# Hymba layer, fp32 in three products: the last output tile's mixed activation blocks made between the products of the first gate/up pair, and the token scale one product later

## The chip, the cores and the metric

The kernel runs on one core of a Trainium2 chip. The metric is the device time of one execution in microseconds; the median of three runs of the kernel before is 2037.42 us (2037.31 to 2037.79).

## The reference

One decoder layer for 512 tokens of width 2048, with 16 learned tokens put ahead of them. Cut to what matters here:

```python
n = _rmsnorm(h, g_mix[l])
p = n @ w_in[l]                       # q, k, v | gb, gc, u
o_attn = _stick_breaking_attention(q, k, v)
o_conv = gb * _causal_dwconv(gc * u, conv_w[l])
o = jnp.concatenate([_rmsnorm(o_attn, g_attn_out[l]),
                     _rmsnorm(o_conv, g_conv_out[l])], axis=-1)
h = h + o @ w_out[l]
n2 = _rmsnorm(h, g_ffn[l])
h = h + (jax.nn.silu(n2 @ w_gate[l]) * (n2 @ w_up[l])) @ w_down[l]
```

## The kernel before

**Precision.** Every operand of a large product is split into a high part and a rest (hi, lo), and a product is three matmuls: hi by hi, hi by lo, lo by hi (lines 795, 796 and 797, each once per tile of 128 rows, so 24 matmuls for one block of eight tiles).

**Pairs.** The projections are done in pairs of 2 x 2 blocks of weights (a gate tile and an up tile in the feed-forward part, and two tiles of the convolution's projections), each pair with seven block products instead of eight. `pair_product` (L799) uses three PSUM banks, x, y and z. The product x(acts[2]) goes on adding to the bank x after the product x(acts[0]) in it was copied out, and so on: after x(acts[0]), z(acts[1]) and x(acts[2]) ScalarE copies the bank into `sides` (`read_out`, L811), and after z(acts[3]) and x(acts[4]) VectorE reads it into `out2` (L825, L829), the two halves of u. The last product, x(acts[6]), adds to the bank x again. Normal pairs go x0, z1, x2, z3, x4, y5, x6. The first convolution pair (i = 0) and the first gate/up pair (i = CONV) are "swapped": the product y(acts[5]) comes first.

**Weights.** A product's weights are made by `prepare` (L225), up to two products ahead (S_AHEAD), in three places of `sw_split` that are used in turn: SP loads a block of 512 KB (`load_quad`, L167), ScalarE rounds it to the high part (L202), VectorE subtracts for the low part (L203). The products 1, 2, 4 and 6 use sums of blocks, made by VectorE: t1 and t3 in `add_quads` (L209), t2 in L252, and t2 with the last block in L219. Each block's load for the next pair is put on SP behind the last sum that reads the block (`load_next`, L183). The steps run at high priority, and a scheduler sets the order in which each engine's queue gets them, unless the code pins it. Seven weights steps of a swapped pair come in the order 5, 0, 1, 2, 3, 4, 6 (L223).

**The output projection's tiles.** They are walked in the order of OUT_TILES (L938). For each, the residual is added (L980 to L984), scaled by g_ffn into `src` (L986), and the blocks of the feed-forward part's seven activations acts[0] to acts[6] are made: plain ones, differences and sums of the four quarter blocks, each split into hi and lo (`split_f`, L990, over L324). Blocks 4 and 6 go through DRAM (`fx`) and are loaded by POOL (`load_f`, L919). For the last tile, i = KT - 1 = 15, with the banks po15x, po15y and po15z, all this runs in one piece at the highest priority (L1007 to L1012): residual, `mixed_blocks` (L997) with acts 0, 1, 2, then 3 and 4, and the sum of squares (L345) for the feed-forward part's norm.

**The token scale.** `h_scale` (L1044) splits that sum (L324, tile work_r), has PE sum it over the partitions (ss_h, L673 and L676), and makes the reciprocal root with VectorE and ScalarE. In the first gate/up pair it is called after the product z(acts[3]) (L826); the result scales g and u in `gate` (L1072).

## Time and profile before

| | us |
|---|---|
| median of three runs | 2037.42 |
| the profiled execution, its own time | 2037.97 |
| its span in the trace | 2036.1 |
| around the span | 1.9 |
| first gate/up pair, first matmul | 767.35 |
| third gate/up pair, first matmul | 811.29 |

PE is TensorE's matmul stream, PEld its weight loads, DVE VectorE, ACT ScalarE, POOL GpSimd, SP the queue that issues the weights' loads. A row of the timeline has the start and the length in us, the engine, the line of the kernel, the operation, out<-in, and the shape; what stands in brackets at its end is the idle time before it and what released it. A row of the waits has the total in us, how often, and the longest. All times of the trace count from the start of the span. The ends of matmuls are modelled (0.28 us of length at a pace of 0.11), so matmuls are timed from start to start.

### The profile page before, as it was taken

The page shows a single profiled execution, that of the slowest core. Times are in us where ns is not written, and L with a number is a line of the kernel's source. Part 1 is how long each engine was busy: PE and PEld are TensorE (multiplying, and loading weights), DVE is VectorE, ACT ScalarE, POOL GpSimd, SP SyncE. Part 2 cuts the span into 40 slices and gives each one's busy share as a digit, 9 for nine tenths or more (in the row PEclk, how much of TensorE's full clock was granted, in tenths as well). Part 3 has the DMA queues.
Part 4 walks back from the last instruction along what each step waited for, and adds up shares of the span by engine and source line. Part 5 has one row for each costly group of instructions (what it writes and reads, how often), then busy time and mean ns, then how long its engine had stood idle before and what let it go on. Part 6 is the DMA issues. An engine that isn't in the chain of part 4 may idle for free.

```text
span 2036.1 us, 39674 instructions
## 1 busy us (share of the span) xinstructions
PE 2022.7 (99%) x16158; PEld 1962.6 (96%) x16158; DVE 1728.1 (85%) x2196; ACT 1078.8 (53%) x1556; POOL 337.9 (17%) x507
## 2 busy tenths in 40 slices
PE   9999999999999999999999999999999999999999
PEld 8999999899998889999999999999999999999999
DVE  7877777698878778998988988988998978888887
ACT  7776766344454445555555555555555544444443
POOL 0111111200014440111111110110110242131211
PEclk9999999999999999999999999999999999999999
DMA  6343344833355556556555555555555999797864
GB/s 221 102 140 123 125 136 136 270 104 107 104 205 175 167 160 203 146 171 181 149 168 160 152 168 157 154 168 156 158 166 153 283 340 349 170 313 200 220 151 89
DMA packets 156087, 356.30 MB, mean 175 GB/s; under 512 B 13632, under 2 KB 67648, under 8 KB 155136
## 3 DMA queue, kind: packets, MB, share of 16 engines
q1 hardware_dynamic: 72208, 216.76, 33.4%
q0 software_dynamic: 83696, 136.99, 25.1%
q8 instruction: 127, 2.08, 0.4%
q14 instruction: 56, 0.46, 0.1%
HBM read 275.78 MB, written 77.92 MB: 174 GB/s over the span
## 4 chain that ended last, share of the span: by engine, by line
PE 92%; DVE 3%; DMA 2%; ACT 1%; issue 1%; POOL 0%; SPq 0%; DVEq 0%; ACTq 0%; POOLq 0%
PE x L795 13%; PE x L797 13%; PE x L796 13%; PE z L795 7%; PE z L796 7%; PE z L797 7%; PE y L796 3%; PE y L797 3%; PE y L795 3%; PE pv L311 2%; PE pv L312 2%; PE pv L313 2%; PE pk L312 1%; PE pk L311 1%; PE pk L313 1%; PE pq L313 1%
## 5 line engine op out<-in xcount | busy, mean ns | idle before, releaser
L202 ACT CAST sw_split<-sw_in 128x1024 fp32r<-128x1024 f32 (+2 forms) x668 | 661.7, 992 | 709.8 <-PE z L796 193.3
L203 DVE TENSOR_TENSOR sw_split<-sw_in,sw_split 128x1024 fp32r<-128x1024 f32 (+2 forms) x668 | 777.8, 1165 | 149.2 <-ACT sw_split L202 144.3
L797 PE MATMUL x<-f,sw_split 128*128 128x256 f32 x1408 | 387.4, 275 | 0.4 <-DVE sw_split L203 0.4
L795 PE MATMUL x<-f,sw_split 128*128 128x256 f32 x1408 | 387.4, 275 | 0.1
L796 PE MATMUL x<-f,sw_split 128*128 128x256 f32 x1408 | 387.3, 275 | 0.0
L797 PEld LDWEIGHTS x<-f,sw_split 128*128 128x128 f32 x1408 | 264.3, 188 | 0.6 <-DVE sw_split L203 0.6
L795 PEld LDWEIGHTS x<-f,sw_split 128*128 128x128 f32 x1408 | 264.3, 188 | 0.5 <-ACT sides L811 0.5
L796 PEld LDWEIGHTS x<-f,sw_split 128*128 128x128 f32 x1408 | 264.3, 188 | 0.0
L1066 POOL DMA_DIRECT2D fd<-s x147 | 103.7, 922 | 710.8 <-DVE s L324 710.0
L209 DVE TENSOR_TENSOR sw_in<-sw_in 128x1024 f32<-128x1024 f32 (+1 forms) x164 | 187.9, 1146 | 13.1 <-DMA sw_in<-w_in 5.0
L797 PE MATMUL z<-f,sw_split 128*128 128x256 f32 x704 | 193.8, 275 | 1.7 <-DVE sw_split L203 1.7
L795 PE MATMUL z<-f,sw_split 128*128 128x256 f32 x704 | 193.9, 275 | 1.5 <-ACT sides L811 1.3
L796 PE MATMUL z<-f,sw_split 128*128 128x256 f32 x704 | 193.7, 275 | 0.0
L797 PE MATMUL x<-ring,sw_split 128*128 128x256 f32 x608 | 167.3, 275 | 0.5 <-DVE sw_split L203 0.5
L795 PE MATMUL x<-ring,sw_split 128*128 128x256 f32 x608 | 167.2, 275 | 0.0
L796 PE MATMUL x<-ring,sw_split 128*128 128x256 f32 x608 | 167.2, 275 | 0.0
L797 PEld LDWEIGHTS z<-f,sw_split 128*128 128x128 f32 x704 | 132.2, 188 | 1.9 <-DVE sw_split L203 1.9
L795 PEld LDWEIGHTS z<-f,sw_split 128*128 128x128 f32 x704 | 132.2, 188 | 1.9 <-ACT sides L811 1.5
L796 PEld LDWEIGHTS z<-f,sw_split 128*128 128x128 f32 x704 | 132.2, 188 | 0.0
L797 PEld LDWEIGHTS x<-ring,sw_split 128*128 128x128 f32 x608 | 114.1, 188 | 0.7 <-DVE sw_split L203 0.7
L795 PEld LDWEIGHTS x<-ring,sw_split 128*128 128x128 f32 x608 | 114.1, 188 | 0.0
L796 PEld LDWEIGHTS x<-ring,sw_split 128*128 128x128 f32 x608 | 114.1, 188 | 0.0
(609 smaller groups left out, 5459.1 us busy)
## 6 DMA issues: line engine op xcount, KB each, us to landing
sw_in<-w_gu SPq DMA_DIRECT2D x176, 512.0 KB, 4.0
sw_in<-w_in SPq DMA_DIRECT2D x92, 512.0 KB, 3.4
fd<-s POOLq DMA_DIRECT2D x147, 256.0 KB, 5.3
sw_in<-w_down SPq DMA_DIRECT2D x96, 384.0 KB, 4.3
ring<-fd POOLq DMA_DIRECT2D x42, 768.0 KB, 16.8
sw_in<-w_out SPq DMA_DIRECT2D x32, 512.0 KB, 3.4
out_T<-d POOLq DMA_DIRECT2D x54, 256.0 KB, 4.7
mix_dram<-st_x POOLq DMA_DIRECT2D x16, 516.0 KB, 4.1
```

The source lines that it names most:

```text
L202: sc.copy(hi, src)
L203: ve.tensor_tensor(lo, src, hi.bitcast(F32), ALU.subtract)
L209: return ve.tensor_tensor(sums[name], a, b, ALU.add)
L311: pe.matmul(ps, wh, ah[:, a:b], start=k + i == 0, stop=False)
L312: pe.matmul(ps, wh, al[:, a:b], start=False, stop=False)
L313: pe.matmul(ps, wl, ah[:, a:b], start=False, stop=k + i == last)
L795: pe.matmul(p, hi[:, kk], ah, start=start and j == k == 0, stop=False, skip_group_check=skip)
L796: pe.matmul(p, hi[:, kk], al, start=False, stop=False, skip_group_check=skip)
L797: pe.matmul(p, lo[:, kk], ah, start=False, stop=k == n - 1, skip_group_check=skip)
L1066: gp.dma_start(fd[c][s][:, :, k], t[:, :, i])
```

## The change

The last tile's three mixed blocks are taken out of the one piece and put into a list, `between`: the third block (L1011 of the new file, for acts[2]), the fourth (L1015, acts[3]) and the fifth (L1021, acts[4], with the sum of squares behind it and the release of the buffers). `go_between` runs one after each of the pair's first three products, at high priority and queued behind `latest[0]`, which is the last low half of weights or the last t2 sum issued till then. The token scale runs after x(acts[4]) instead of after z(acts[3]). The pool that holds its work tiles opens when the fifth block is done, so g and u get a pool of their own. In the swapped pairs, both of them, the t3 sum and the last sum (with the loads behind them) are also queued behind `latest[0]`. The other output tiles run the same operations as before.

```diff
--- before.py
+++ after.py
@@ -151,6 +151,7 @@
     pieces += [("pair", i, s) for i in range(CONV, len(pairs)) for s in range(7)]
     quads, sums, split_w, used, wide, raws = {}, {}, [], [0], {}, []
     S_AHEAD = 2
+    latest = [None]
 
     def load_first(i):
 
@@ -200,7 +201,7 @@
             at = half * 8 * P
             hi, lo = (sw_split[:, at + i * 4 * P : at + (i * 4 + n) * P] for i in range(2))
         sc.copy(hi, src)
-        ve.tensor_tensor(lo, src, hi.bitcast(F32), ALU.subtract)
+        latest[0] = ve.tensor_tensor(lo, src, hi.bitcast(F32), ALU.subtract)
         split_w.append((hi, lo))
 
     def add_quads(i, name, a, b):
@@ -249,13 +250,14 @@
             elif s == 1:
                 split_quad(sums["t1"], n)
                 sums["t2"] = sums["t1"]
-                ve.tensor_tensor(sums["t2"], sums["t2"], b["22"], ALU.add)
+                latest[0] = ve.tensor_tensor(sums["t2"], sums["t2"], b["22"], ALU.add)
                 if not swapped:
                     add_t3(i, b)
             elif s == 2:
                 split_quad(sums["t2"], n)
                 if swapped:
-                    add_t3(i, b)
+                    with tc.issue_after(latest[0].ins):
+                        add_t3(i, b)
             elif s == 3:
                 split_quad(b["22"], n)
                 load_next(i, "22")
@@ -267,7 +269,8 @@
                     add_last(i, b)
             else:
                 if swapped:
-                    add_last(i, b)
+                    with tc.issue_after(latest[0].ins):
+                        add_last(i, b)
                 split_quad(sums["t2"], n)
                 if i + 1 == SIX:
                     load_quad(SIX + 1, QUADS[1])
@@ -796,7 +799,14 @@
                 pe.matmul(p, hi[:, kk], al, start=False, stop=False, skip_group_check=skip)
                 pe.matmul(p, lo[:, kk], ah, start=False, stop=k == n - 1, skip_group_check=skip)
 
-    def pair_product(acts, cols, out2, side, fourth=None):
+    between = []
+
+    def go_between():
+        if between:
+            with tc.high_priority(), tc.issue_after(latest[0].ins):
+                between.pop(0)()
+
+    def pair_product(acts, cols, out2, side, fifth=None):
 
 
 
@@ -815,18 +825,21 @@
         first = i in (0, CONV)
         if first:
             block_product(y, acts[5], True)
+            go_between()
         block_product(x, acts[0], True)
         read_out(p1, x)
+        go_between()
         block_product(z, acts[1], True)
+        go_between()
         read_out(p5, z)
         block_product(x, acts[2], False)
         read_out(u2, x)
         block_product(z, acts[3], False)
         ve.scalar_tensor_tensor(out2[0], z, -1.0, u2, ALU.mult, ALU.subtract)
-        if fourth:
-            fourth()
         block_product(x, acts[4], False)
         ve.scalar_tensor_tensor(out2[1], x, -1.0, p5, ALU.mult, ALU.subtract)
+        if fifth:
+            fifth()
         if not first:
             block_product(y, acts[5], True)
         return y, lambda: (block_product(x, acts[6], False), x)[1]
@@ -994,29 +1007,38 @@
             ve.tensor_tensor(src[:, 4], src[:, 3], src[:, 1], ALU.subtract)
             split_f(1, 4)
 
-        def mixed_blocks():
-            split_f(0, 0)
-            if i < KT - 1:
-                late_block()
+        def third_block():
             ve.scalar_tensor_tensor(src[:, 4], src[:, 4], -1.0, src[:, 0], ALU.mult, ALU.subtract)
             split_f(2, 4)
+
+        def fourth_block():
             ve.scalar_tensor_tensor(src[:, 5], src[:, 4], -1.0, src[:, 2], ALU.mult, ALU.subtract)
+            if i < KT - 1:
+                ve.tensor_tensor(src[:, 1], src[:, 0], src[:, 1], ALU.subtract)
+            split_f(3, 5)
+
+        def fifth_block():
             ve.tensor_tensor(src[:, 1], src[:, 0], src[:, 1], ALU.subtract)
+            split_f(4, 1)
+            square_sum(acc_h, hj, False, wide_tmp("h", bufs=2), ve)
+            hbuf.release()
+            nonlocal apool
+            apool = open_pool("apool")
 
         if i == KT - 1:
             with tc.high_priority(1 << 20):
                 residual(ve)
-                mixed_blocks()
-                split_f(3, 5)
-                split_f(4, 1)
-                square_sum(acc_h, hj, False, wide_tmp("h", bufs=2), ve)
+                split_f(0, 0)
+            between.extend([third_block, fourth_block, fifth_block])
         else:
             residual(gp if half else ve)
             if half:
                 split_f(5, 2)
             else:
-                mixed_blocks()
-                split_f(3, 5)
+                split_f(0, 0)
+                late_block()
+                third_block()
+                fourth_block()
             st = two(wide_tmp("st", F32R, 2))
             split(st[:, 0], st[:, 1], src[:, 3 if half else 1])
             gp.dma_start(fx[6 if half else 4][:, :, k], st)
@@ -1028,18 +1050,17 @@
         (gp if i < KT - 1 else nc.sync).dma_start(out[j], hj)
     assert not waiting
     acts = [acts[s] for s in range(7)]
-    hbuf.release()
-
-    def ffn_pair(acts, c1, c2, fourth=None):
+
+    def ffn_pair(acts, c1, c2, fifth=None):
 
         cols = c1.shape[-1]
         side = [sides[:, n * T2 : n * T2 + cols] if cols == T2 or not n else c2[:, 2 - n] for n in range(3)]
         views = [lambda part, k, t=t: t[:, part, k] for t in acts]
-        y, last = pair_product(views, cols, [c2[:, t] for t in range(2)], side, fourth)
+        y, last = pair_product(views, cols, [c2[:, t] for t in range(2)], side, fifth)
         ve.tensor_tensor(c1[:, 0], y, side[0], ALU.add)
         return last()
 
-    apool = open_pool("apool")
+    gu_pool = open_pool("gu_pool")
 
     def h_scale():
         w = apool.tile([P, 5, SEQ], F32R, tag="s5", name="work_r")
@@ -1104,8 +1125,8 @@
                 gp.dma_start(rings[c, s][:, part], fd[c][s][:, part], max_dma_last_dim=3072)
 
     for f in range(FT):
-        g1 = apool.tile([P, 2, T2], F32, tag="c1", name=f"g{f}")
-        u1 = apool.tile([P, 2, T2], F32, tag="c2", name=f"u{f}")
+        g1 = gu_pool.tile([P, 2, T2], F32, tag="c1", name=f"g{f}")
+        u1 = gu_pool.tile([P, 2, T2], F32, tag="c2", name=f"u{f}")
         x = ffn_pair(acts, g1, u1, None if f else h_scale)
         if f < FT - 1:
             gate(f, g1, u1, x)
@@ -1122,6 +1143,7 @@
     pad(first, 11936 - 8192)
     gate(FT - 1, g1, u1, x)
     apool.release()
+    gu_pool.release()
     fpool_last.release()
     cpool = open_pool("cpool")
     d = cpool.tile([P, 4, SEQ], F32, name="d")
```

The numbers of operations stay as they were on every engine, and POOL's and SP's transfers too; POOL's order is unchanged. What moves is shown at three places.

VectorE, from the last residual operation of the last output tile (L984 before, L997 after; f_6616, f_6615, f_6617, f_6614 and f_7874 are acts 1, 0, 2, 3 and 4, src is the tile's quarter blocks, sw_in and sw_split the weights). Before:

```order
L984 TENSOR_TENSOR w_7895<-w_7895,sw_in 128x256
L209 TENSOR_TENSOR sw_in<-sw_in 128x1024
L1001 TENSOR_SCALAR src_7878<-src_7878 128x256
L324 TENSOR_TENSOR f_6615<-src_7878,f_6615 128x256
L1003 TENSOR_SCALAR src_7878<-src_7878 128x256
L324 TENSOR_TENSOR f_6617<-src_7878,f_6617 128x256
L1004 TENSOR_TENSOR src_7878<-src_7878 128x256
L324 TENSOR_TENSOR f_6614<-src_7878,f_6614 128x256
L345 TENSOR_TENSOR acc_h<-acc_h,w_7919 128x512
L324 TENSOR_TENSOR f_7874<-src_7878,f_7874 128x256
L203 TENSOR_TENSOR sw_split<-sw_in,sw_split 128x1024
L324 TENSOR_TENSOR work_r<-acc_h,work_r 128x512
```

After:

```order
L997 TENSOR_TENSOR w_7895<-w_7895,sw_in 128x256
L204 TENSOR_TENSOR sw_split<-sw_in,sw_split 128x1024
L253 TENSOR_TENSOR sw_in<-sw_in 128x1024
L327 TENSOR_TENSOR f_6615<-src_7878,f_6615 128x256
L1011 TENSOR_SCALAR src_7878<-src_7878 128x256
L204 TENSOR_TENSOR sw_split<-sw_in,sw_split 128x1024
L1015 TENSOR_SCALAR src_7878<-src_7878 128x256
L210 TENSOR_TENSOR sw_in<-sw_in 128x1024
L204 TENSOR_TENSOR sw_split<-sw_in,sw_split 128x1024
L1021 TENSOR_TENSOR src_7878<-src_7878 128x256
L327 TENSOR_TENSOR f_6617<-src_7878,f_6617 128x256
L327 TENSOR_TENSOR f_6614<-src_7878,f_6614 128x256
```

In the new order the weights' low halves (L204), the t2 sum (L253) and the t3 sum (L210) stand between the blocks, where before all the blocks stood ahead of the first of them.

VectorE around the first pair's last products (g and u are its results, work_r the token scale's split, work_a and work_b its work tiles). Before:

```order
L203 TENSOR_TENSOR sw_split<-sw_in,sw_split 128x1024 x2
L219 TENSOR_TENSOR sw_in<-sw_in 128x1024
L203 TENSOR_TENSOR sw_split<-sw_in,sw_split 128x1024
L677 TENSOR_SCALAR work_a<-ss_h 128x512
L203 TENSOR_TENSOR sw_split<-sw_in,sw_split 128x1024
L209 TENSOR_TENSOR sw_in<-sw_in 128x1024
L335 TENSOR_SCALAR work_b<-work_b,work_a 128x512
L825 TENSOR_SCALAR u_7956<-z_7958,sides 128x256
L336 TENSOR_SCALAR acc_h<-work_b,work_a 128x512
L829 TENSOR_SCALAR u_7956<-x_7959,sides 128x256
L203 TENSOR_TENSOR sw_split<-sw_in,sw_split 128x1024 x2
```

After:

```order
L348 TENSOR_TENSOR acc_h<-acc_h,w_8039 128x512
L204 TENSOR_TENSOR sw_split<-sw_in,sw_split 128x1024
L220 TENSOR_TENSOR sw_in<-sw_in 128x1024
L327 TENSOR_TENSOR f_7874<-src_7878,f_7874 128x256
L1060 TENSOR_TENSOR g_7942<-y_7944,sides 128x256
L204 TENSOR_TENSOR sw_split<-sw_in,sw_split 128x1024
L327 TENSOR_TENSOR work_r<-acc_h,work_r 128x512
L838 TENSOR_SCALAR u_7943<-z_7945,sides 128x256
L204 TENSOR_TENSOR sw_split<-sw_in,sw_split 128x1024
L210 TENSOR_TENSOR sw_in<-sw_in 128x1024
L840 TENSOR_SCALAR u_7943<-x_7946,sides 128x256
L680 TENSOR_SCALAR work_a<-ss_h 128x512
```

The sum of squares and the fourth activation's low half come down among the weights' steps; the read-out of x into u (L829, now L840) comes ahead of the token scale's reading of ss_h (L677, now L680) instead of behind its end.

TensorE ahead of the first pair's last product (x10 and z10 are banks of the first gate/up pair, x11 and z11 of the second; f6 is acts[6], f0 acts[0]). Before:

```order
L796 MATMUL x11_8190<-f0_6615,sw_split_119 128x256
L797 MATMUL x11_8190<-f0_6615,sw_split_119 128x256
L795 MATMUL z11_8189<-f1_6616,sw_split_119 128x256
L796 MATMUL z11_8189<-f1_6616,sw_split_119 128x256
L795 MATMUL x10_7959<-f6_7875,sw_split_119 128x256
L796 MATMUL x10_7959<-f6_7875,sw_split_119 128x256
```

After:

```order
L800 MATMUL x10_7946<-f4_7874,sw_split_119 128x256
L676 MATMUL ss_h_8137<-work_r_8132,ones_r_110 128x512
L679 MATMUL ss_h_8137<-work_r_8132,ones_r_110 128x512
L798 MATMUL x11_8193<-f0_6615,sw_split_119 128x256
L799 MATMUL x11_8193<-f0_6615,sw_split_119 128x256
L800 MATMUL x11_8193<-f0_6615,sw_split_119 128x256
L798 MATMUL x11_8193<-f0_6615,sw_split_119 128x256
L799 MATMUL x11_8193<-f0_6615,sw_split_119 128x256
L798 MATMUL x10_7946<-f6_7875,sw_split_119 128x256
L799 MATMUL x10_7946<-f6_7875,sw_split_119 128x256
```

The sums of squares now stand behind the product x(acts[4]) and not ahead of it. Before, the whole next x(acts[0]), 24 matmuls from row 5138 to 5161, and two of the next z(acts[1]) stand ahead of x(acts[6]); now five matmuls of that x(acts[0]) do, and its other 19 follow behind.

VectorE in the first convolution pair (cu and sides_c are its results). Before:

```order
L203 TENSOR_TENSOR sw_split<-sw_in,sw_split 128x1024
L839 TENSOR_TENSOR sides_c<-y_4462,sides_c 128x256
L203 TENSOR_TENSOR sw_split<-sw_in,sw_split 128x1024
L209 TENSOR_TENSOR sw_in<-sw_in 128x1024
L203 TENSOR_TENSOR sw_split<-sw_in,sw_split 128x1024
L209 TENSOR_TENSOR sw_in<-sw_in 128x1024
L825 TENSOR_SCALAR cu_4461<-z_4463,sides_c 128x258
L203 TENSOR_TENSOR sw_split<-sw_in,sw_split 128x1024
```

After:

```order
L852 TENSOR_TENSOR sides_c<-y_4462,sides_c 128x256
L204 TENSOR_TENSOR sw_split<-sw_in,sw_split 128x1024
L220 TENSOR_TENSOR sw_in<-sw_in 128x1024
L210 TENSOR_TENSOR sw_in<-sw_in 128x1024
L838 TENSOR_SCALAR cu_4461<-z_4463,sides_c 128x258
L204 TENSOR_TENSOR sw_split<-sw_in,sw_split 128x1024 x2
L210 TENSOR_TENSOR sw_in<-sw_in 128x1024
L204 TENSOR_TENSOR sw_split<-sw_in,sw_split 128x1024
```

Before, a sum of the next pair (the first L209 of these rows) stands ahead of the low half for x(acts[4]) (the L203 behind it). After, that low half (the L204 behind L852) stands ahead of the pair's own last sum (L220) and of the next pair's first sum (the first L210). The pair's t3 sum, at row 488 before and thus among the projections ahead of this pair, is now at row 499, behind the low half for x(acts[2]).

## The prediction

> **What bounds the kernel now.** I read the head of the profile page and its chain first.
>
> ```profile
> span 2036.1 us, 39674 instructions
> PE 2022.7 (99%) x16158; PEld 1962.6 (96%) x16158; DVE 1728.1 (85%) x2196; ACT 1078.8 (53%) x1556; POOL 337.9 (17%) x507
> PE 92%; DVE 3%; DMA 2%; ACT 1%; issue 1%; POOL 0%; SPq 0%; DVEq 0%; ACTq 0%; POOLq 0%
> ```
>
> TensorE is busy 99% of the span, and the change takes no matmul away. So it can only give back time in which PE stands. The diff touches two places, the last output tile with the first gate/up pair and, by the two new waits in the weights' step for the swapped pairs, the first convolution pair as well. I therefore read PE's waits in two windows, 740 to 830 us and 380 to 480 us.
>
> ```profile
> PE z L797 <- DVE sw_split L203: 1.7, 1, 1.7
> PE z L795 <- ACT sides L811: 1.3, 1, 1.3
> PE x L797 <- DVE sw_split L203: 0.4, 1, 0.4
> PE z L795 <- ACT sw_split L202: 0.2, 1, 0.2
> ```
>
> ```profile
> PE x L797 <- DVE sw_split L203: 1.2, 1, 1.2
> PE x L795 <- ACT sw_split L202: 1.0, 1, 1.0
> ```
>
> These are the only prizes, 3.7 us in the first window and 2.2 us in the second. Then PE's timeline, with a steady pair (the fourth row, from the table of windows: length, then busy PE, PEld, DVE, ACT, POOL) for comparison.
>
> ```profile
> 767.35 0.28 PE L795 MATMUL y<-f,sw_split 128*128 128x256 f32 x1
> 774.98 0.39 PE L797 MATMUL z<-f,sw_split 128*128 128x256 f32 x1 [1.74 <-DVE sw_split L203]
> 779.07 0.39 PE L795 MATMUL z<-f,sw_split 128*128 128x256 f32 x1 [1.29 <-ACT sides L811]
> ```
>
> ```profile
> 784.70 0.40 PE L673 MATMUL ss_h<-work_r,ones_r 128*128 128x512 f32 x1
> 785.40 0.39 PE L795 MATMUL x<-f,sw_split 128*128 128x256 f32 x1
> 811.29 0.28 PE L795 MATMUL x<-f,sw_split 128*128 128x256 f32 x1
> ```
>
> ```profile
> 830.33:849.37 19.04, 19.04 (x170) 19.04 (x169) 17.03 (x20) 9.71 (x13) 1.40 (x2) 1.00 0.59 177
> 849.37:868.41 19.04, 19.04 (x170) 19.04 (x169) 18.26 (x22) 10.26 (x13) 3.54 (x5) 1.00 0.51 143
> ```
>
> A steady pair has 168 matmuls in 19.04 us, 0.1133 each, so a product of 24 takes 2.72. From the first product of the first gate/up pair (767.35) to the start of the third pair (811.29) there are 336 of them, 38.08 us, and the two sums of squares, 785.40 - 784.70 = 0.70. That makes 38.78 of 43.94 us: **5.16 us are lost**, the waits and the slow restart behind each.
>
> **Why PE waits there.** VectorE's and ScalarE's timelines tell it.
>
> ```profile
> 769.15 0.43 DVE L984 TENSOR_TENSOR w<-w,sw_in 128x256 f32<-128x256 f32 x1
> 769.62 1.22 DVE L209 TENSOR_TENSOR sw_in<-sw_in 128x1024 f32<-128x1024 f32 x1
> 770.76 0.42 DVE L1001 SCALAR_TENSOR_TENSOR src<-src 128x256 f32<-128x256 f32 x1
> 771.10 0.42 DVE L324 TENSOR_TENSOR f<-src,f 128x256 fp32r<-128x256 f32 x1
> ...
> 773.71 1.21 DVE L203 TENSOR_TENSOR sw_split<-sw_in,sw_split 128x1024 fp32r<-128x1024 f32 x1
> 774.85 0.68 DVE L324 TENSOR_TENSOR work_r<-acc_h,work_r 128x512 fp32r<-128x512 f32 x1
> 775.45 1.21 DVE L203 TENSOR_TENSOR sw_split<-sw_in,sw_split 128x1024 fp32r<-128x1024 f32 x1
> ```
>
> ```profile
> 777.70 1.04 ACT L202 CAST sw_split<-sw_in 128x1024 fp32r<-128x1024 f32 x1 [2.32 <-PE z L796]
> ```
>
> The low half of the weights for z(acts1) is made at 773.71 only, behind all the mixed blocks; PE asked for it near 773.1. The late products then hold back a cast, and the copy of z queues behind that cast (the 1.29). From start to start a wide operation (1024 columns) takes 1.14 us, 1.13 to the hundredth in most places, one of 512 takes 0.60 and a narrow one (256) 0.34, mostly 0.33.
>
> **The change, first gate/up pair.** No operation is added or removed; the same ones run in the order of the rows shown with the change. I laid that order out from one narrow step after L984, at 769.48. Up to the second half of u0 (L840 of the new file), on which x(acts6) waits because it accumulates on the bank that L840 reads, VectorE has ten wide steps (11.3), nine narrow (3.0), two of 512 (1.2), an in-place wait of 0.1, and two places where it waits for ScalarE's 1.04 us cast of a sum that it has just made (t2, and t2 + b21), about 0.55 each: 16.7 us. L840 starts at 786.2 and ends 0.42 later, at 786.6.
> In between, each low half is ready in time: z(acts1)'s by 770.7 (PE needs it at 773.1), x(acts2)'s by 774.3 (775.8), z(acts3)'s by 776.9 (778.5), x(acts4)'s by 779.7 (781.2). The activations' last tile is read by the last three matmuls of a product, and is tight: act0 772.3 against 772.6, act2 777.6 against 778.0; the rest has 2 us or more. So both waits of 1.74 and 1.29 go. PE runs six products from 767.35 to 783.7 and the sums of squares to 784.4.
> What is late next: the order then puts five matmuls of the next pair ahead of x(acts6). The third needs a low half made at 784.0 to 785.2, so PE stands 0.6; after them it waits for L840 from 785.5 to 786.7, **a new wait of 1.2 us**. In before the whole next x(acts0), 24 matmuls, stood there and covered it. From 786.7 on there are 187 matmuls, 21.2 us, and 0.2 for the restart: the third pair starts at 808.1 instead of 811.3. **Term one: -3.2 us** (the later waits of 0.4 and 0.2 are among it).
> The rule of the Trainium skill that bears on this is in "TensorE: Matmul & The Clock Gate", section "Part 2: What happens when you issue a matmul": only weight loads are pulled ahead, the matmuls stay in program order, so the 19 ready matmuls of the next pair don't pass the waiting one. The waits at 774.98 and 779.07, with ready work queued behind them, agree; if matmuls could pass, 19 x 0.1133 = 2.2 us would cover the new wait and this term would be -4.4.
>
> Moved loads. The load of the next pair's block b12 is queued on SP behind the new place of the t3 sum, and leaves at 775.9 instead of 770.9. Its landing time in before, then one issued near 777.9, then the median (KB each, us to landing):
>
> ```profile
> sw_in<-w_gu SPq DMA_DIRECT2D x1, 512.0 KB, 9.2
> ```
>
> ```profile
> sw_in<-w_gu SPq DMA_DIRECT2D x1, 512.0 KB, 6.7
> ```
>
> ```profile
> sw_in<-w_gu SPq DMA_DIRECT2D x176, 512.0 KB, 4.0
> ```
>
> It is needed by the sum t1 at 785.1, so it has 9.2 us. Bounds: early by 5 us, or, at the 9.2 of before, just in time. I take no cost, by the neighbour's 6.7, issued at nearly the same time. SP and POOL issue the same transfers in number, and POOL in the same order.
>
> **The change, first convolution pair.** Here VectorE and PE now:
>
> ```profile
> 403.47 1.23 DVE L209 TENSOR_TENSOR sw_in<-sw_in 128x1024 f32<-128x1024 f32 x1 [2.86 <-DMA sw_in<-w_in]
> ```
>
> ```profile
> 404.40 0.28 PE L797 MATMUL z<-mixed,sw_split 128*128 128x258 f32 x1
> 405.89 0.39 PE L797 MATMUL x<-n,sw_split 128*128 128x258 f32 x1 [1.21 <-DVE sw_split L203]
> ```
>
> A sum that waits 2.86 us for a load stands ahead of x(acts4)'s low half, which PE then awaits. In the new order the low half stands ahead of the sum, is made from 401.3 to 402.5, and PE goes on at 404.5: 405.89 - 404.5 = **term two: -1.4 us**. The wait of 1.0 for the cast stays, since the slot it writes comes free with z(acts1) as before. Bounds: 0, if the load below spoils it, and 1.5, the 405.89 - 404.40 that the two rows lie apart; I take 1.4, since one matmul's 0.11 of that is work. Here too the next pair's b12 load leaves later, at 394.9 instead of 372.6; it is needed at 403.5. Loads of before, issued at those times:
>
> ```profile
> sw_in<-w_in SPq DMA_DIRECT2D x1, 512.0 KB, 3.2
> ```
>
> ```profile
> sw_in<-w_in SPq DMA_DIRECT2D x1, 512.0 KB, 6.6
> ```
>
> At 6.6 it lands at 401.5, 2 us early; with a slower one the margin is gone from 8.6 on.
>
> **Sum.** -3.2 - 1.4 = -4.6 us. The profiled execution took 2037.97 us, its span 2036.1 and 1.9 around it; it would take 2033.4 and span 2031.5. It lies 0.55 above the median of 2037.42, against which the forecast is **2032.8 us**.
>
> **Rivals.**
> A, VectorE becomes the bound of the pairs behind. First the two pairs together and a piece of the second, then the read-outs on which x(acts6) of the first and of the second pair waited:
>
> ```profile
> 767.30:811.30 44.00, 40.23 (x341) 39.00 (x341) 39.46 (x52) 24.16 (x36) 4.26 (x6) 1.00 0.65 214
> 792.00:798.00 6.00, 5.57 (x49) 5.37 (x49) 6.00 (x7) 2.77 (x5) 0.00 (x0) 1.00 0.17 45
> ```
>
> ```profile
> 790.66 0.41 DVE L829 SCALAR_TENSOR_TENSOR u<-x,sides 128x256 f32<-128x256 f32 x1
> ...
> 807.19 0.42 DVE L829 SCALAR_TENSOR_TENSOR u<-x,sides 128x256 f32<-128x256 f32 x1
> ```
>
> The same 39.5 us of VectorE must now fit into 40.8, and from 792 to 798 it had no idle time already. A steady pair leaves it 0.8 to 2.0 us, so a backlog shrinks slowly. For it: PE would want the second read-out by 808.1 - 2.72 = 805.4, 2.2 us before the 807.6 at which it ended. The first one ends at 786.6 instead of 791.1, 4.5 us sooner, but three operations of the token scale, 1.8 us, that stood ahead of it now come behind: VectorE is 2.7 us ahead of before, a margin of 0.5 us. Against it: the places where it stood idle in before, 44.00 - 39.46 = 4.5 us, can be filled by the new order. Price, by what part of those 4.5 us it keeps idle beyond my table, 0.6 to 2.5 us: -4.0 to -2.1, so 2033.4 to 2035.3, and 2034.3 in the middle.
> B, the moved convolution load lands late, at 8.6 us or more; the sum then heads VectorE's queue and term two is gone: -3.2, 2034.2.
> C, slower: the narrow operations now spread to 784 meet a POOL that uses the same memory.
>
> ```profile
> 754.87 1.51 DVE L1001 SCALAR_TENSOR_TENSOR src<-src 128x256 f32<-128x256 f32 x1
> ```
>
> ```profile
> 754.14 1.95 POOL L981 TENSOR_TENSOR w<-w,sw_in 128x512 f32<-128x512 f32 x1
> ```
>
> ```profile
> 767.34 2.86 POOL L921 DMA_DIRECT2D f<-fx  x4 [2.71 <-PE po15z L774]
> ```
>
> Beside a POOL addition L1001 took 1.51 instead of 0.42. Each such case adds 1.09 us to the chain that ends in L840; five cost the gain (5.5 against 4.6), eight make the kernel slower by 4.1 us, nine by 5.2: 2042.6. Against it: POOL only issues transfers there, and L984 at 769.15 took 0.43 beside them.
> "SBUF — State Buffer" of the Trainium skill, section "SBUF: two separate sides", says that such a VectorE operation with two inputs and a GpSimd operation that reads SBUF lock one pair of ports in turn; the 1.51 beside the 1.95 agrees.
> D, the wait for x(acts6) is hidden too, if VectorE's hand-overs overlap better than I laid them: -5.8, 2031.6.
> E, the change does nothing, because the order comes out as before: 2037.4. The order rows speak against it.
>
> **How the numbers follow.** Forecast 0.52, A 0.24, B 0.10, C 0.06, D 0.05, E 0.03. A measurement of this kernel can tell about 0.2%, 4.07 us, from no change, so the border lies at 2033.35, close to the forecast. Faster: forecast and D, 0.57. Same: A, B and E, 0.37. Slower: C, 0.06. The range takes in D (2031.6, less 0.1), and A to its bound (2035.3) and half a us for A and B together: 2031.5 to 2035.8.
>
> **What would show it.** Right: in the first gate/up pair no wait of z for a low half or for a copy; one wait of about 1.2 us of x(acts6) near 785.5; third pair at 808; in the convolution pair the wait of 1.2 gone, the 1.0 kept. Wrong: waits in the second gate/up pair or later (A), a sum waiting for a load ahead of 404 (B), narrow operations over 1 us long (C), or x(acts6) without a wait (D).

## The result and the profile after

The changed kernel takes **2031.97 us** (median of 9 runs, 2031.55 to 2033.02) against 2037.42 (median of 9, 2036.21 to 2037.97): 5.45 us less, a ratio of 0.9973 with a 95% interval of 0.9965 to 0.9982. The forecast was 2032.8, and the time lies inside the range. The profiled execution took 2032.01 us, its span 2030.2, which is 5.9 less than that of before.

The head of the page and the chain of the changed kernel:

```profile
span 2030.2 us, 39679 instructions
PE 2020.8 (100%) x16158; PEld 1961.8 (97%) x16158; DVE 1727.2 (85%) x2196; ACT 1078.7 (53%) x1556; POOL 337.8 (17%) x507
PE 95%; DVE 3%; ACT 1%; issue 1%; DMA 1%; SPq 0%; ACTq 0%; DVEq 0%
```

PE has the same matmuls, and its share of the span rose (2022.7 of 2036.1 us before, 2020.8 of 2030.2 now) because idle time went. PE's waits from 740 to 830 us, and then from 380 to 480 us:

```profile
PE x L798 <- DVE u L840: 0.9, 1, 0.9
PE x L800 <- DVE sw_split L204: 0.5, 1, 0.5
```

```profile
PE x L798 <- ACT sw_split L203: 1.1, 1, 1.1
```

The four waits of before (3.7 us, two in the first gate/up pair and two in products of the second) are gone, and two new ones of 1.4 us are there. In the convolution pair the 1.2 is gone and the 1.0 stays (1.1 now). Gone too is a wait of 0.2 us for the mixed activations, which was not forecast. It is the third row of the same view of before:

```profile
PE z L795 <- DMA mixed<-mix_dram: 0.2, 1, 0.2
```

PE's timeline of the gate/up stage:

```profile
765.00 0.28 PE L798 MATMUL y<-f,sw_split 128*128 128x256 f32 x1
...
782.74 0.38 PE L800 MATMUL x<-f,sw_split 128*128 128x256 f32 x1 [0.49 <-DVE sw_split L204]
...
784.21 0.39 PE L798 MATMUL x<-f,sw_split 128*128 128x256 f32 x1 [0.85 <-DVE u L840]
...
805.72 0.28 PE L798 MATMUL x<-f,sw_split 128*128 128x256 f32 x1
```

From the first product to the third pair it is 805.72 - 765.00 = 40.7 us instead of 43.9: 3.2 us less. VectorE's chain of operations behind it, from the last residual operation to the read-out on which x(acts6) waits:

```profile
766.49 0.43 DVE L997 TENSOR_TENSOR w<-w,sw_in 128x256 f32<-128x256 f32 x1
766.84 1.22 DVE L204 TENSOR_TENSOR sw_split<-sw_in,sw_split 128x1024 fp32r<-128x1024 f32 x1
768.09 1.23 DVE L253 TENSOR_TENSOR sw_in<-sw_in 128x1024 f32<-128x1024 f32 x1
...
782.60 1.22 DVE L210 TENSOR_TENSOR sw_in<-sw_in 128x1024 f32<-128x1024 f32 x1
783.73 0.42 DVE L840 SCALAR_TENSOR_TENSOR u<-x,sides 128x256 f32<-128x256 f32 x1
```

From L997 to L840 it is 17.24 us; the hand-made order gave 786.2 - 769.15 = 17.05. The convolution stage, from its first product to the next pair's third (216 matmuls), before and after:

```profile
387.98 0.28 PE L795 MATMUL y<-n,sw_split 128*128 128x258 f32 x1
...
398.56 0.39 PE L795 MATMUL z<-mixed,sw_split 128*128 128x258 f32 x1 [0.23 <-DMA mixed<-mix_dram]
...
401.28 0.39 PE L795 MATMUL x<-n,sw_split 128*128 128x258 f32 x1 [1.02 <-ACT sw_split L202]
...
417.40 0.28 PE L795 MATMUL x<-mixed,sw_split 128*128 128x258 f32 x1
```

```profile
387.56 0.28 PE L798 MATMUL y<-n,sw_split 128*128 128x258 f32 x1
...
400.40 0.38 PE L798 MATMUL x<-n,sw_split 128*128 128x258 f32 x1 [1.06 <-ACT sw_split L203]
...
403.63 0.28 PE L800 MATMUL x<-n,sw_split 128*128 128x258 f32 x1
...
415.05 0.28 PE L798 MATMUL x<-mixed,sw_split 128*128 128x258 f32 x1
```

It takes 27.5 us instead of 29.4: 1.9 less. From the first matmul of x(acts4) to its third, the one that waited, it is 403.63 - 400.40 = 3.23 instead of 405.89 - 401.28 = 4.61: 1.4. The remainder, 0.5, is for the most part the wait for the mixed activations: the 24 steps up to the matmul that waited there take 2.98 us instead of 3.37. So the two stages give 5.1 of the 5.9. The other 0.8 lies where nothing was changed (0.4 ahead of the convolution pair, 0.3 behind the gate/up stage); over the 14 profiles of this study the first of these stretches ends between 387.1 and 388.3 us and the last takes 1224.2 to 1225.2, so it is scatter between executions.

### The profile page after: what moved, and what is told of

The parts are those of the page before. It is cut to its first block, busy times and chain, and to the rows that moved or that the text cites. A ratio compares the mean times of both kernels' runs of the same rounds, so it can differ in the third digit from the quotient of the medians.

```text
span 2030.2 us, 39679 instructions
## 1 busy us (share of the span) xinstructions
PE 2020.8 (100%) x16158; PEld 1961.8 (97%) x16158; DVE 1727.2 (85%) x2196; ACT 1078.7 (53%) x1556; POOL 337.8 (17%) x507
## 4 chain that ended last, share of the span: by engine, by line
PE 95%; DVE 3%; ACT 1%; issue 1%; DMA 1%; SPq 0%; ACTq 0%; DVEq 0%
PE x L798 13%; PE x L800 13%; PE x L799 13%; PE z L799 7%; PE z L798 7%; PE z L800 7%; PE y L799 3%; PE y L798 3%; PE y L800 3%; PE pv L314 2%; PE pv L315 2%; PE pv L316 2%; PE pq L316 1%; PE pq L314 1%; PE pq L315 1%; PE pk L315 1%
## 5 line engine op out<-in xcount | busy, mean ns | idle before, releaser
L203 ACT CAST sw_split<-sw_in 128x1024 fp32r<-128x1024 f32 (+2 forms) x668 | 661.9, 992 | 704.2 <-PE z L799 187.1
L204 DVE TENSOR_TENSOR sw_split<-sw_in,sw_split 128x1024 fp32r<-128x1024 f32 (+2 forms) x668 | 777.8, 1165 | 147.1 <-ACT sw_split L203 142.6
L210 DVE TENSOR_TENSOR sw_in<-sw_in 128x1024 f32<-128x1024 f32 (+1 forms) x164 | 187.9, 1146 | 9.0 <-DMA sw_in<-w_down 2.1
```

Source lines behind the costliest of these rows:

```text
L203: sc.copy(hi, src)
L204: latest[0] = ve.tensor_tensor(lo, src, hi.bitcast(F32), ALU.subtract)
L210: return ve.tensor_tensor(sums[name], a, b, ALU.add)
```

## The experiments

All times are medians, with the kernel before at 2037.1 to 2037.4 beside them. The last columns are from the profiles: the convolution stage (216 matmuls from its first product), the gate/up stage (338 from its first product, the two sums of squares included), the start of VectorE's chain (the last residual operation behind the first gate/up product), and the gate/up stage less that start.

| kernel | time | less than before | conv. stage | gate/up stage | start | stage - start |
|---|---|---|---|---|---|---|
| before | 2037.42 | | 29.41 | 43.94 | 1.81 | 42.13 |
| changed | 2031.97 | 5.45 | 27.49 | 40.73 | 1.50 | 39.23 |
| e1 convolution part alone | 2035.18 | 2.1 | 27.48 | 43.70 | 1.53 | 42.17 |
| e2 gate/up part alone | 2034.05 | 3.3 | 29.21 | 40.34 | 1.15 | 39.19 |
| e3 sums not queued | 2032.43 | 4.9 | 27.50 | 41.05 | 1.72 | 39.33 |
| e4 scale early | 2032.32 | 5.0 | 27.49 | 40.81 | 1.21 | 39.60 |
| e5 read-out first | 2032.49 | 4.7 | 27.53 | 40.99 | 1.62 | 39.37 |
| e6 convolution order | 2032.47 | 4.7 | 27.75 | 41.25 | 2.04 | 39.21 |
| e7 both of these | 2032.30 | 4.8 | 27.74 | 40.37 | 1.00 | 39.37 |
| e8 squares on POOL | 2032.40 | 4.7 | 27.51 | 41.09 | 1.64 | 39.45 |
| e9 load later (the program of e2) | 2034.14 | 3.2 | 29.45 | 40.69 | 1.65 | 39.04 |
| e10 copy first | 2033.83 | 3.5 | 27.31 | 40.54 | 1.32 | 39.22 |
| e11 two more | 2033.44 | 3.9 | 27.50 | 41.81 | 1.38 | 40.43 |
| e12 changed again | 2032.09 | 5.3 | 27.50 | 40.75 | 1.58 | 39.17 |

The theory is that the order of VectorE's queue makes the gain, in two stages whose gains add. The rivals are that the token scale's later place makes it, that the moved loads make it, and that VectorE's backlog bounds what follows.

**e1 and e2, each part alone.** In e1 the kernel before gets the queued sums for pair 0 only, in e2 the changed kernel loses them there:

```diff
             elif s == 2:
                 split_quad(sums["t2"], n)
                 if swapped:
-                    with tc.issue_after(latest[0].ins):
+                    with tc.issue_after(latest[0].ins) if i == CONV else contextlib.nullcontext():
                         add_t3(i, b)
```

(and the same for the last sum; e1 has `i == 0` and nothing else of the change.)

> The kernel before with only the two new waits in the first convolution pair's weights steps; the last output tile, the first gate/up pair and the token scale stay as before. Theory (VectorE's order sets both gains, and they add): PE's wait of 1.2 us for the low half of x(acts4) is gone, the wait of 1.0 for the cast stays, the time is 1.5 us below before (1.9 if the 0.2 us wait for the mixed load goes with it); the first gate/up pair loses its 5.2 us as before. Rival (all of the gain is in the gate/up pair): no difference.

> The changed kernel without the two new waits in the first convolution pair; all else as changed. Theory: -3.2 us against before (43.9 us from the first gate/up product to the third pair become 40.7), and the convolution pair shows its 1.2 us wait again; with the other part alone the two sums make -4.7, so that some 0.7 of the measured -5.45 is scatter or comes from elsewhere. Rival (the parts work on each other through the loads' places): the two alone add up to something clearly else than the whole.

PE's waits of e1 from 740 us on (the two longest of four), and of e2 in the convolution pair:

```profile
PE z L804 <- DVE sw_split L204: 1.5, 1, 1.5
PE z L802 <- ACT sides L818: 1.3, 1, 1.3
```

```profile
PE x L800 <- DVE sw_split L204: 1.2, 1, 1.2
PE x L798 <- ACT sw_split L203: 1.0, 1, 1.0
```

Each part removes its own waits and leaves the other's. They give 2.1 and 3.3 us (ratios 0.9989, interval 0.9981 to 0.9998, and 0.9986, 0.9977 to 0.9994). The sum, 5.4, is close to the 5.45 of the whole, but each interval is 3.5 us wide. That the parts add is shown by the stages: e1 has the changed kernel's convolution stage (27.48) with a gate/up stage like that of before (43.70), e2 the other way round (29.21 and 40.34). The sum expected was 4.7; most of the difference is in e1, whose stage gains 1.9 and not 1.5.

**e3, the gate/up pair's sums not queued** (`i == CONV` becomes `i == 0` in the lines above).

> The changed kernel without the two new waits in the first gate/up pair: its t3 sum and its last sum go back ahead of the low halves; blocks and token scale stay where the change put them. Theory (the chain of VectorE's operations up to the read-out of x into u bounds the pair): a wait of about 1.3 us appears at x(acts2) or z(acts3), because the low half of act2's last tile is made later, but x(acts6) starts at the same time, its wait shrinks by as much, and the time is within 0.5 us of the changed kernel. Rival (the queued sums are what removes the waits): the early wait adds to the late one, 1.3 to 2 us slower than the changed kernel.

PE's waits of e3:

```profile
PE x L799 <- DVE f L327: 1.3, 1, 1.3
```

The wait of 1.3 us appears at x(acts2), as expected, the wait for the read-out is no longer among the waits (0.42 us from one matmul to the next is left of it), and the stage less its start is 39.33 instead of 39.2. An early wait and a late one did not add up. What sets the end of the pair is VectorE's chain of operations up to the read-out, wherever on the way PE waits for it. So it is the blocks between the products that make the gate/up gain; to queue the sums as well is worth 0.1 us in the stage, and 0.5 between the medians, of which the traces place only the 0.1. Nor does the moved load make the gain here: in e3 the load of b12 leaves 3.4 us behind the first product again, as in before (3.5; 8.2 in the changed kernel), and the gain stays.

**e4, the token scale early again.**

```diff
+        if fifth:
+            fifth()
         block_product(x, acts[4], False)
         ve.scalar_tensor_tensor(out2[1], x, -1.0, p5, ALU.mult, ALU.subtract)
-        if fifth:
-            fifth()
```

> The changed kernel with the token scale called after z(acts3) again, ahead of x(acts4). Theory (order of the blocks makes the gain, the scale's place only keeps PE from waiting for its split): PE waits some 2.5 us for the split of the sum of squares ahead of x(acts4), x(acts6) then starts 0.9 us later than in the changed kernel, and the time is 0.9 us (0.5 to 1.5) above the changed kernel, 4.5 below before. Rival (the later token scale makes the gain): 3 us or more above the changed kernel.

```profile
PE ss_h L676 <- ACT work_r L327: 0.8, 1, 0.8
PE ss_h L679 <- DVE work_r L327: 0.3, 1, 0.3
```

PE waits for the split, 1.1 us and not 2.5, and the time is 0.35 above the changed kernel, not 0.9. The sign is as expected and the size a third of it. The rival is refuted: the scale's later place makes at most 0.4 of the 3.2 us.

**e5, the read-out ahead of the next pair's sum.** `later` keeps the t1 sum and its load for the pair behind the first one.

```diff
-        ve.scalar_tensor_tensor(out2[1], x, -1.0, p5, ALU.mult, ALU.subtract)
+        read_x = ve.scalar_tensor_tensor(out2[1], x, -1.0, p5, ALU.mult, ALU.subtract)
+        if i == CONV:
+            with tc.high_priority(), tc.issue_after(read_x.ins):
+                later.pop()()
```

> The changed kernel with the next pair's t1 sum (and its load) queued behind the read-out of x into u, instead of ahead of it; the scheduler then puts two, not five, of the next pair's matmuls ahead of x(acts6). Theory (x(acts6) waits for that read-out at the end of VectorE's chain): the read-out starts 1.13 us sooner, x(acts6) too, and the time is 1.1 us below the changed kernel. Rival (VectorE's backlog bounds the pairs behind): the gain is given back in the second or third pair, within 0.3 us of the changed kernel.

PE's row of x(acts6) in e5, and the busy times over 20 us behind it (length, then PE, PEld, DVE, ACT, POOL), in e5 and in the changed kernel:

```profile
783.20 0.38 PE L803 MATMUL x<-f,sw_split 128*128 128x256 f32 x1 [0.94 <-DVE u L845]
```

```profile
786.00:806.00 20.00, 19.81 (x169) 19.22 (x168) 19.97 (x24) 12.30 (x17) 1.41 (x2) 1.00 0.46 147
```

```profile
785.00:805.00 20.00, 20.00 (x177) 19.95 (x176) 19.64 (x24) 12.86 (x18) 1.40 (x2) 1.00 0.46 134
```

x(acts6) starts 1.0 us sooner than in the changed kernel (18.18 against 19.21 behind the first product, with three matmuls fewer ahead of it), and nothing of it is left: the stage less its start is 39.37, and the time not below the changed kernel's. VectorE is busy 19.97 of 20.00 us, and PE stands three times for 0.2 to 0.3 us in the second pair, as in this step from 791.40 to 791.77, too short to be named in the list of waits:

```profile
791.40 0.28 PE L804 MATMUL x<-f,sw_split 128*128 128x256 f32 x1
791.77 0.39 PE L805 MATMUL x<-f,sw_split 128*128 128x256 f32 x1
```

My theory of this run failed, and the rival, that the second pair gives the gain back, is what the run shows. The full queue is only part of it, since the order in it changed as well. One more low half now stands ahead of the second pair's read-out, which starts 37.15 us behind the last residual operation, against 35.82 in the changed kernel:

```profile
801.72 1.21 DVE L204 TENSOR_TENSOR sw_split<-sw_in,sw_split 128x1024 fp32r<-128x1024 f32 x1
...
803.79 0.41 DVE L845 SCALAR_TENSOR_TENSOR u<-x,sides 128x256 f32<-128x256 f32 x1
```

In the changed kernel's profile the margin is already used up: the second pair's read-out and the matmul that needs it stand there as

```profile
802.31 0.42 DVE L840 SCALAR_TENSOR_TENSOR u<-x,sides 128x256 f32<-128x256 f32 x1
```

```profile
802.72 0.28 PE L800 MATMUL y<-f,sw_split 128*128 128x256 f32 x1
802.88 0.35 PE L798 MATMUL x<-f,sw_split 128*128 128x256 f32 x1
```

that is 0.16 from one matmul to the next instead of 0.11.

**e6, e7 and e10, the wait that stays in the convolution pair.** In e6 the first matmul of x(acts4) of pair 0 is kept in program order, behind z(acts3); e7 has e5's edit as well; e10 has e6's and queues the cast behind the copy of z(acts1).

```diff
-        block_product(x, acts[4], False)
+        block_product(x, acts[4], False, i == 0)
...
+            elif s == 4 and i == 0:
+                with tc.issue_after(copied[0].ins):
+                    split_quad(sums["t3"], n)
```

> The changed kernel with x(acts4) of the first convolution pair kept behind z(acts3) on PE, where two of its matmuls now stand ahead and wait 1.1 us for their cast. Theory (PE's own order makes that wait): the 1.1 wait is gone; VectorE's low halves for the next products come at 404.2 to 406.5 as before and become the bound, so that a wait of 0.5 to 0.8 us comes back behind x(acts4): 0.4 to 0.8 us below the changed kernel. Rival (the cast bounds in any order): no difference.

> The edits of the last two kernels together. Theory: they are in different stages and add: 1.5 to 1.9 us below the changed kernel, 7 below before.

> The changed kernel with, in the first convolution pair, x(acts4) kept behind z(acts3) on PE and the cast for it queued behind ScalarE's copy of z(acts1). Theory (z(acts3) waits for that copy, which stands behind the 1.04 us cast): the wait of 1.3 of the last try shrinks to about 0.4 us, and the stage from the first convolution product on takes 0.5 us less than in the changed kernel (27.5). Rival (VectorE's low halves for the next products are the bound): a wait comes back behind x(acts4), the stage takes 27.4 or more.

PE's waits in e6, and in e10:

```profile
PE z L798 <- ACT sides_c L823: 1.3, 1, 1.3
```

```profile
PE y L805 <- DVE sw_split L204: 0.8, 1, 0.8
PE z L801 <- ACT sides_c L826: 0.5, 1, 0.5
PE x L801 <- DVE cu L845: 0.3, 1, 0.3
PE y L801 <- ACT sw_split L203: 0.2, 1, 0.2
```

All three missed. In e6 the 1.1 us wait for the cast only changes its name: z(acts3) now waits 1.3 for ScalarE's copy, which stands behind that cast, and the stage takes 0.25 us more. e10 removes most of that (0.5 left) and the stage takes 27.3, but 1.75 us are lost in the convolution pairs behind it, most of it where a cast and a low half now come late (0.2 and 0.8 in the list). e7 gives no gain either (2032.30). None of these kernels beats the changed one.

**e8, the squares' addition on POOL.**

```diff
-            square_sum(acc_h, hj, False, wide_tmp("h", bufs=2), ve)
+            square_sum(acc_h, hj, False, wide_tmp("h", bufs=2), gp)
```

> The changed kernel with the addition of the last tile's squares (128 x 512) on POOL instead of VectorE: a step of 0.6 us leaves VectorE's chain, and an addition of about 1.95 us runs on POOL beside it. Theory of the third rival (a POOL operation and a VectorE operation with two inputs hold each other up): one or more VectorE operations beside it take 1 us longer or more, the read-out of x into u comes 0.5 us later or more, 0.3 to 1.3 us above the changed kernel. If they don't hold each other up: the read-out comes 0.6 us sooner and the time is 0.6 us below the changed kernel.

VectorE's and POOL's rows in e8:

```profile
769.31 1.52 DVE L327 TENSOR_TENSOR f<-src,f 128x256 fp32r<-128x256 f32 x1
770.76 0.41 DVE L1011 SCALAR_TENSOR_TENSOR src<-src 128x256 f32<-128x256 f32 x1
```

```profile
768.22 2.33 POOL L348 TENSOR_TENSOR acc_h<-acc_h,w 128x512 f32<-128x512 f32 x1 [0.43 <-ACT w L347]
```

The narrow subtraction that meets POOL's addition takes 1.52 us, the narrow operation behind it 0.41: one such meeting costs 1.1 us and outweighs the 0.6 us step that was taken from VectorE. The stage less its start is 0.25 longer than in the changed kernel, the time 0.4. So the third rival's price was right, and only its condition is absent in the changed kernel, where POOL only issues transfers, the last until 767.9. The rule of the Trainium skill in "SBUF — State Buffer", section "SBUF: two separate sides", that such a pair of operations takes turns on one pair of ports, agrees with the 1.52 beside the 2.33.

**e9, the load of b12 written behind that of b21.** (The blocks b11 to b22 are the four of a pair's weights.)

```diff
-        load_next(i, "12")
+        if i:
+            load_next(i, "12")
...
         load_next(i, "21")
+        if not i:
+            load_next(i, "12")
```

> The kernel with the gate/up part alone (the convolution pair's sums not queued), in which only the load of the next pair's block b12 is put behind the load of b21, so that it leaves at about 395 us instead of 372.6. Theory (the moved load takes traffic away from the load of the mixed activations, on which PE waited 0.2 us in before): the 0.2 wait near 398.5 goes and the two half products ahead of it take 2.98 us from start to start, as in each kernel with the queued sums, not 3.15 or 3.37; the 1.2 us wait for the low half stays; 0.2 to 0.4 us below the gate/up part alone. Rival (the queued sums themselves or chance): 3.15 or more.

The edit moved nothing. The scheduler put the load back in its old place, and e9 is the same program as e2, instruction by instruction. The load of b12 leaves behind the t3 sum in both, in e9 and in e2:

```profile
371.82 0.33 SPq L175 DMA_DIRECT2D sw_in<-w_in  x1
```

```profile
372.69 0.33 SPq L175 DMA_DIRECT2D sw_in<-w_in  x1
```

So neither the theory nor its rival was tested, and what e9 shows is how far two executions of one program differ. The wait for the mixed activations is gone here without a moved load: the 24 steps up to it take 2.98 us in e9, 3.15 in e2 and 3.37 in before. In the eleven profiles with the queued sums they take 2.98 to 3.00.

What does go with the queued sums in every profile is an earlier landing of the last of the six loads of the mixed activations: 18.0 to 18.8 us behind its issue in these eleven, 19.3 to 20.1 in before, e2 and e9. On SP's queue the load of b12 leaves just ahead of those six in the three, and some 20 us later in the eleven. Its 512 KB, at the 408 GB/s that the DMA engines moved in before from 384 to 400 us, are 1.3 us of transfer, an estimate of the size of the difference. No run moves that load alone, though, so the cause is argued and not shown.

The other thing to see in e9 is that without the queued sums this wait costs nothing: the stage takes 29.21 to 29.45 in before, e2 and e9, and most in e9, which lacks the wait. The next sum heads VectorE's queue and waits for a load until 403.0. VectorE's row, and PE's wait behind it:

```profile
403.13 1.23 DVE L210 TENSOR_TENSOR sw_in<-sw_in 128x1024 f32<-128x1024 f32 x1 [2.89 <-DMA sw_in<-w_in]
```

```profile
405.55 0.39 PE L803 MATMUL x<-n,sw_split 128*128 128x258 f32 x1 [1.74 <-DVE sw_split L204]
```

PE's wait is 1.7 instead of 1.2, the stage 29.45 against 29.21 in e2, and the time is that of e2.

**e11, two operations more in the chain, and e12, the changed kernel again.** In e11 the low halves of acts 3 and 4 are subtracted twice.

```diff
             split_f(4, 1)
+            for s, b in ((3, 5), (4, 1)):
+                hi, lo = acts[s][:, 0, k], acts[s][:, 1, k]
+                ve.tensor_tensor(lo, src[:, b], hi.bitcast(F32), ALU.subtract)
```

> The changed kernel with two narrow subtractions made twice (acts 3 and 4, last tile), which gives the same values; the read-out of x into u then also falls behind the token scale's first step. VectorE's chain up to that read-out is 0.67 + 0.60 = 1.27 us longer. Theory (the stage is the start of that chain behind the first product plus 39.2 us): from the first gate/up product to the third pair it takes the start plus 40.5 us. Rival (there is slack in the chain, PE bounds): plus 39.2 to 39.6.

> The changed kernel once more, unchanged. Theory: the start of VectorE's chain (the end of the last residual operation's start behind the first product) differs from execution to execution between 1.0 and 2.0 us, and the stage takes that start plus 39.2 us (39.0 to 39.4); the convolution stage takes 27.5 us. Rival: the stage takes 40.7 us whatever the start.

PE's waits of e11:

```profile
PE x L798 <- DVE u L840: 1.8, 2, 1.2
PE z L799 <- DVE f L1025: 0.2, 1, 0.2
```

e12 gives 39.17 and e11 40.43, the numbers expected, but e11 came to its number by another way. The read-out was only 0.7 us later, because 0.6 of the added work fitted into VectorE's wait for a cast, and seven more matmuls of the next pair, 0.8 us, now stand ahead of x(acts6) and cover that. The 1.2 us are lost at the second pair's read-out (the longer of the two waits), which has one low half more ahead of it in VectorE's queue than in the changed kernel. So the agreement with 40.5 is luck, and e11 does not test the sum of the chain. Over the six executions with the new chain as it is (changed and e12, which are one program, e2 and e9, which are another, e6 and e10) the start of the chain lies between 1.15 and 2.04 us, and the stage less it between 39.04 and 39.23: the stage follows the start one to one. What is left to win there is an earlier start, or work taken from VectorE; of the 40.7 us, 38.78 are PE's own work.

## Why the prediction was right

- **What bounds, and that only waits can be won.** Right: the stage gains are in the two places named, and e1 and e2 each show one of them alone. The list of waits lacked one row, the 0.2 us for the mixed activations.
- **Term one, -3.2.** The stage went from 43.94 to 40.73. At the same start of the chain it is 42.15 to 39.2, so 2.9 of it is the order's and 0.3 is the earlier start in that execution: that 3.2 was met so closely is in part luck. The waits of 1.74 and 1.29 went as said. The one for the read-out came, 0.85 against the 1.2 forecast; from start to start the two gaps there, 0.76 and 1.13 instead of 0.11, lose 1.7 against the 1.8 forecast. The case in which the 19 ready matmuls of the next pair pass the waiting one (-4.4) did not come: PE started none of them between 783.07 and 784.21.
- **Term two, -1.4.** The wait's own gain is 1.4 as forecast, but the stage gained 1.9. What was mis-sized is when PE comes to x(acts4). The prediction took it from before, with the wait for the mixed activations ahead of it; in the changed kernel that wait is gone, and PE is there 0.4 us sooner. That the load of b12 no longer leaves ahead of those activations is the likely reason, but e9, which was to show it, is the program of e2, so the cause stays open. These 0.5 us are most of the gap between -4.6 and -5.45. No trace places the rest, and the interval of the ratio, 3.7 to 7.1 us, takes in both numbers.
- **Rival A, the backlog.** It did not take the gain, but its margin was mis-sized: 0.5 us by my sum, none in the trace (0.16 instead of 0.11 from matmul to matmul at 802.72). In e5 and e11 the second pair's read-out is where the time is lost, each time with one low half more ahead of it.
- **Rival B.** Absent: the sum at 402.66 waited for no load.
- **Rival C.** The price was right, 1.1 us a meeting (e8); its condition did not occur.
- **Rival D.** Its time, 2031.6, lies nearer to the measured one than the forecast does, but its sign did not come: x(acts6) waits.
- **The rival that the scale's move makes the gain** was not priced in the prediction; e4 gives it 0.4 at most.
- **The chances.** The point lay 0.5 us from the border at 0.2%. The measured ratio is 0.27% below one; its interval (0.18 to 0.35%) reaches the border, so the runs do not settle on which side of it the gain lies.

## What to carry to other kernels

When one engine's queue holds back another, write the queue down in its new order with the durations of the trace, and follow it to the last operation for which the other engine waits: that sum was within 0.2 us here, and where the waits on the way stood did not matter (e3). A gain on the waiting engine is lost again at the next place where the same queue has no margin, so look for that place before shortening anything further (e5, e7). An edit that moves a line of the program need not move the operation, since the scheduler orders the queues: read the new order in the trace before reading the time (e9), and where the order changed elsewhere too, the time measures that as well (e5, e11).

## What the runs showed of the hardware

A stall can be too short for the list of waits and still cost. In e5 a matmul starts three times 0.31 to 0.37 us behind the one before it, instead of 0.11; as the record of a matmul is 0.28 us long, less than 0.1 of idle time is left to be seen. The matmul behind it then follows after 0.22, as behind the long waits (784.21 to 784.43 in the changed kernel). The three stalls, 1.0 us together, gave back what e5 had gained.

The start of VectorE's chain behind PE's first product differed by 1.0 us between the executions of the changed kernel and its variants (1.00 to 2.04), by 0.5 between two of the same program (1.15 in e2, 1.65 in e9), and over the six executions named above the stage's time followed it. What sets that start was not tried.
